# Strassen-Winograd halves in the MLP's second product: seven products instead of eight per quarter

## The chip, the cores and the metric

The kernel runs on one NeuronCore of a Trainium2 chip. Five engines work side by side, each through its own queue: TensorE (PE, matrix products; its weight loads are shown apart as PEld), VectorE (DVE), ScalarE (ACT), GpSimd (POOL) and SyncE (SP), which here issues the DMAs. They wait for each other through semaphores. The metric is the device time of one execution in microseconds, lower is better.

## The reference

A decoder block over 512 tokens of 1024 features: two attention-like branches are merged and added to the residual stream `x`, then an MLP with a squared ReLU, then gated input embeddings, then a last norm. What matters here is the part behind the branches:

```python
x = x + merged @ w_out[i]
h = rms_norm(x, mlp_norm_g[i])
x = x + jnp.square(jax.nn.relu(h @ w_ff1[i])) @ w_ff2[i]
gate = jax.nn.sigmoid(rms_norm(x, ple_norm_g[i]) @ w_ple_gate[i])
x = x + gate * (p[i] @ w_ple_proj[i])
...
return rms_norm(x, final_norm_g)
```

`w_ff1` is 1024 x 4096, `w_ff2` 4096 x 1024, all in float32.

## The kernel before

**Precision.** A float32 factor is split in two: `hi`, rounded by ScalarE to the short format that TensorE takes (fp32r), and `lo`, the remainder, by VectorE (`split`; for weights in `fetch_to`, L172 and L173). Every product is three matmuls: hi times hi, hi times lo, lo times hi.

**Weights** come in units of 128 x 1024 numbers (512 KB). The list `seq` (L126 to L145) fixes the order of all 132 units. `load_to` issues a unit's DMA on SyncE into `w_raw` (two buffers), `fetch_to` splits it into `w_hi` and `w_lo` (three buffers each). `weights(u, i)` takes the next unit; at the third `step()` within it, `fetch_to` prepares two units further on (L196).

**The MLP** (from L1081) runs in four quarters of 1024 hidden features. In a quarter, the first product makes eight tiles of 128 hidden features by 512 tokens, each from one unit of `U_FF1` (`product`, `mm3`, L188 to L190: 24 matmuls). `squared` (L1096) takes relu times the norm's factor on VectorE, the square on ScalarE, and splits the result into `f`. The second product, `by_token` with `U_FF2` (L1116), has 8 units for the quarter; for each half of 512 output columns, four units are multiplied with four tiles of 128 tokens (`rows3`, L203 to L205: 24 matmuls a unit, the activations stationary, 512 weight columns moving), and four VectorE additions put the sums from PSUM into `xs` (L1118). PSUM has eight banks of 128 x 512, taken in turn by `ps_main`.

**Around it.** Before the MLP, `embeddings(0, "mlp_g")` makes the first 512 columns of `p @ w_ple_proj` into the SBUF tile `ple`, two token tiles at a time, each pair followed by `gained`: 16 transposes on TensorE (L1021) and the splits of the transposed stream into `hx` (L1025, L1026). `norm_of` makes the norm's factors; `spread` (L1087) spreads them over partitions. Behind the MLP, `embeddings(1, "ple_g")` does the second half, and the gate's product (`U_GATE`) and the end follow. `wg`, a home for the last four split units of the gate, lies in the buffers of `f`.

**Order and memory.** The instructions of the text are put in order for each engine before the run, by readiness as a model of the program sees it and by the program's order; an engine then executes its list strictly in that order. A memory pool that is opened where a closed one lay waits until that one's tiles are done with.

Of the kernel before, what the change touches and what calls it, by code (L numbers as in the profile page):

```python
# [18 lines left out]
P = 128  # L19
T = 512  # L20
D = 1024
KT = D // P
# [25 lines left out]
NUNITS = _n  # L48
# [37 lines left out]
def tile_block(ctx: ExitStack, tc: tile.TileContext, xT, xt, pT, wts, lora, cols_d, gfin_d, consts_d, out, dbg=None):  # L86
    nc = tc.nc
    act, dve, pool, pe, sync = nc.scalar, nc.vector, nc.gpsimd, nc.tensor, nc.sync
# [7 lines left out]
    const = ctx.enter_context(tc.tile_pool(name="const", bufs=1))  # L96
    wpool = ctx.enter_context(tc.tile_pool(name="wpool", bufs=3))
    dpool = ctx.enter_context(tc.tile_pool(name="dpool", bufs=1, space=DRAM))

    o_sb = dpool.tile([P, HP, T], F32, name="o_sb")  # L100
    gates = dpool.tile([P, 2 * KT, T], F32, name="gates")
# [5 lines left out]
    omm = const.tile([P, 14], F32, name="omm")  # L107

    const.tile([P, PAD], F32, name="pad")
    w2a2 = const.tile([P, 512], F32, name="w2a2")  # L110
    g2 = const.tile([P, 512], F32, name="g2")

    def cc(k, w):
        return cst[:, COFF[k]:COFF[k] + w]
# [11 lines left out]
    seq = []  # L126
# [19 lines left out]
    assert len(seq) == NUNITS  # L146
    ready, loaded = {}, []
    state = {"i": 0, "used": 0, "due": 0}
    AHEAD = 3
    homes = {}  # L150

    def unit(i):
        return wts[UBASE[seq[i][0]] + seq[i][1]]

    def load_to(n):
        while len(loaded) < min(n, len(seq)):
            raw = wpool.tile([P, 1024], F32, name="w_raw", bufs=2)
            sync.dma_start(out=raw, in_=unit(len(loaded)))
            loaded.append(raw)

    def fetch_to(n, ahead=0):
        while state["i"] < min(n, len(seq)):
            i = state["i"]
            state["i"] += 1
            load_to(i + 1 + ahead)
            raw = loaded[i]
            if seq[i] in homes:
                hi, lo = homes[seq[i]]()
            else:
                hi = wpool.tile([P, 1024], F32R, name="w_hi")  # L170
                lo = wpool.tile([P, 1024], F32R, name="w_lo")
            act.copy(out=hi, in_=raw)  # L172
            dve.tensor_tensor(out=lo, in0=raw, in1=r32(hi), op=ALU.subtract)  # L173
            ready.setdefault(seq[i], []).append((hi, lo))

    def weights(u, i):
        assert seq[state["used"]] == (u, i), (seq[state["used"]], u, i)
        state["used"] += 1
        fetch_to(state["used"])
        state["due"] = 3  # L180
        return ready[(u, i)].pop(0)

    def mm3(ps, w, base, rhs, k, first, last, t=slice(0, T)):

# [13 lines left out]
    def rows3(ps, w, rhs, tt, k, first, last, cs=slice(0, 512)):  # L198

        xh, xl = (r[:, :, tt * P:(tt + 1) * P] for r in rhs)  # L200
        for j in range(2):
            wh, wl = (p_.rearrange("p (j f) -> p j f", j=2)[:, j, cs] for p_ in w)
            pe.matmul(ps, xh[:, k + j], wh, start=first and j == 0, stop=False)  # L203
            pe.matmul(ps, xh[:, k + j], wl, start=False, stop=False)  # L204
            pe.matmul(ps, xl[:, k + j], wh, start=False, stop=last and j == 1)  # L205
            step()

    def product(ps, w, rhs, nk=KT, base=0, t=slice(0, T)):
# [8 lines left out]
    def split(hi, lo, src):  # L217
        act.copy(out=hi, in_=src)
        dve.tensor_tensor(out=lo, in0=src, in1=r32(hi), op=ALU.subtract)
# [43 lines left out]
    pr = ctx.enter_context(tc.tile_pool(name="pr", bufs=1, side="right"))  # L263
    o_rw = pr.tile([P, HP, T], F32, name="o_rw")
# [4 lines left out]
    with ExitStack() as sA:  # L269
# [43 lines left out]
        with ExitStack() as s1:  # L313
# [12 lines left out]
            ps = ps_z()  # L326
# [41 lines left out]
            first = p1.tile([P, 4 * P], F32, name="first", tag="sums", bufs=1)  # L368
# [150 lines left out]
            pss = [psm.tile([P, T], F32, name="ps_m") for _ in range(2)]  # L519
# [15 lines left out]
                projected(0, i, pss[i])  # L535
            for _ in v:
                pass
            sync.dma_start(out=w2a2, in_=lora[:, 0:512])
            sync.dma_start(out=g2, in_=lora[:, 512:1024])

            def early():
                for hp in range(1, HP):
# [27 lines left out]
        with ExitStack() as s2:  # L570
# [423 lines left out]
    ple = px.tile([P, TT, D], F32, name="ple")  # L994
    pin = [px.tile([P, 2, T], F32R, name=f"pin{i}") for i in range(2)]
    px.tile([P, PADX], F32, name="padx")
    COLHALF = (slice(0, 512), slice(512, D))

    ps4 = ctx.enter_context(tc.tile_pool(name="ps4", bufs=6, space=PSUM))
# [14 lines left out]
    def gained(gname, half):  # L1014

        for kp in range(KT // 2):
            ps = ps_main().rearrange("p (j t) -> p j t", j=2)
            for j in range(2):
                for t in range(2):
                    k = kp * 2 + j  # L1020
                    pe.transpose(out=ps[:, j, t * P:(t + 1) * P], in_=xs[:, half * 2 + t, k * P:(k + 1) * P], identity=ident)  # L1021
            for j in range(2):
                k = kp * 2 + j
                t2 = slice(half * 256, half * 256 + 256)
                act.activation(out=hx[0][:, k, t2], in_=ps[:, j], func=AF.Copy, scale=col(gname, k))  # L1025
                dve.scalar_tensor_tensor(out=hx[1][:, k, t2], in0=ps[:, j], scalar=col(gname, k), in1=r32(hx[0][:, k, t2]),  # L1026
                                         op0=ALU.mult, op1=ALU.subtract)

    def embeddings(half, gname):

        pss = [ps_main() for _ in range(TT)]
        w = weights(U_PLE, half)
        for part in range(2):
            for tt in (part * 2, part * 2 + 1):
                rows3(pss[tt], w, pin, tt, 0, True, True)
                act.copy(out=ple[:, tt, COLHALF[half]], in_=pss[tt])
            gained(gname, part)

    def norm_of(pool_, name):

        st = pool_.tile([P, 3, TT], F32, name=name)
        sq = pool_.tile([P, D], F32, name="sqj", bufs=2)
        for tt in range(TT):
            act.activation(out=sq, in_=xs[:, tt, :], func=AF.Square, accum_out=st[:, 0, tt:tt + 1])
        dve.tensor_scalar(out=st[:, 0, :], in0=st[:, 0, :], scalar1=1.0 / D, scalar2=NORM_EPS, op0=ALU.mult, op1=ALU.add)
        root(st[:, 1, :], st[:, 2, :], st[:, 0, :])
        return st[:, 1, :]

    with ExitStack() as s3:
# [6 lines left out]
        for m in range(8):  # L1056
# [10 lines left out]
            ps = ps_main()  # L1067
# [10 lines left out]
    sP.close()  # L1078


    p4 = ctx.enter_context(tc.tile_pool(name="p4", bufs=1))  # L1081
    f = [p4.tile([P, KT, T], F32R, name=f"f{i}", tag=f"f{i}") for i in range(2)]
    embeddings(0, "mlp_g")
    r2 = norm_of(p4, "st2")
    rs2 = p4.tile([P, T], F32, name="rs2")

    def spread():  # L1087

# [4 lines left out]
            pe.matmul(ps[:, tt * P:(tt + 1) * P], onesd, dg, start=True, stop=True)  # L1093
        act.copy(out=rs2, in_=ps)

    def squared(ps, m):  # L1096
        r = p4.tile([P, T], F32, name="relu", bufs=3)
        dve.scalar_tensor_tensor(out=r, in0=ps, scalar=0.0, in1=rs2, op0=ALU.max, op1=ALU.mult)  # L1098
        act.activation(out=r, in_=r, func=AF.Square)
        split(f[0][:, m, :], f[1][:, m, :], r)  # L1100

    for qd in range(4):
        waiting = []
        for m in range(8):
            w = weights(U_FF1, qd * 8 + m)
            ps = ps_main()
            product(ps, w, hx)
            waiting.append((ps, m))
            if qd == 0 and m < 2:
                continue  # L1110
            if qd == 0 and m == 2:
                spread()
            while waiting:
                squared(*waiting.pop(0))
        for half in range(2):
            pss = by_token(U_FF2, qd * 8, f, half)  # L1116
            for tt in range(TT):
                dve.tensor_tensor(out=xs[:, tt, COLHALF[half]], in0=pss[tt], in1=xs[:, tt, COLHALF[half]], op=ALU.add)  # L1118


    gfin = p4.tile([P, D], F32, name="gfin")
    sync.dma_start(out=gfin, in_=gfin_d)
    wg = [p4.tile([P, 4, 1024], F32R, name=f"wg{i}", tag=f"f{i}") for i in range(2)]
    for kk in range(4):
        homes[(U_GATE, 4 + kk)] = lambda kk=kk: [t[:, kk, :] for t in wg]
# [116 lines left out]
```

## Time and profile before

| | us |
|---|---|
| median of 3 runs (911.72 to 912.33) | 912.2 |
| the profiled execution | 912.86 |
| its span, first to last instruction | 911.1 |
| first matmul of the MLP's second product, quarter 0 | 543.94 |
| end of the four quarters (first matmul of the embeddings' second half) | 848.58 |

A row of a group names line, engine, operation, output and inputs with their shapes, the count, busy time in us and the mean of one in ns, and the engine's idle time ahead of these with what ended it. A row of a stretch gives its bounds and length, then for PE, PEld, DVE, ACT and POOL the busy time with the number of instructions, the clock that TensorE was granted, the DMA engines' busy share and GB/s. A row in order of time gives start and duration in us, engine, line and operation, and in brackets the wait ahead of it. A row of a DMA gives the count, KB each and the median us from issue to landing. SPq is SyncE's queue.

### The profile page before, as it was taken

The page shows a single profiled execution, that of the slowest core. Times are in us where ns is not written, and L with a number is a line of the kernel's source. Part 1 is how long each engine was busy: PE and PEld are TensorE (multiplying, and loading weights), DVE is VectorE, ACT ScalarE, POOL GpSimd, SP SyncE. Part 2 cuts the span into 40 slices and gives each one's busy share as a digit, 9 for nine tenths or more (in the row PEclk, how much of TensorE's full clock was granted, in tenths as well). Part 3 has the DMA queues.
Part 4 walks back from the last instruction along what each step waited for, and adds up shares of the span by engine and source line. Part 5 has one row for each costly group of instructions (what it writes and reads, how often), then busy time and mean ns, then how long its engine had stood idle before and what let it go on. Part 6 is the DMA issues. An engine that isn't in the chain of part 4 may idle for free.

```text
span 911.1 us, 12423 instructions
## 1 busy us (share of the span) xinstructions
PE 893.6 (98%) x4758; PEld 724.3 (79%) x4758; DVE 576.7 (63%) x1086; ACT 416.0 (46%) x682; POOL 82.5 (9%) x137
## 2 busy tenths in 40 slices
PE   8999999999999999999999999999999999999995
PEld 5778788877787877877888888888888888888885
DVE  6899987886978969867835643344334334433666
ACT  6888878535336244344515441144123322321743
POOL 1333322003203112020000000000000000000000
PEclk9999999999999999999999999999999999999998
DMA  7221122220221223448732223332233322233222
GB/s 257 94 78 50 59 81 81 70 92 25 85 79 36 85 90 115 153 129 269 261 114 94 93 93 95 103 103 93 94 94 104 103 93 93 93 94 112 72 70 92
DMA packets 31306, 93.14 MB, mean 102 GB/s; under 512 B 3600, under 2 KB 3600, under 8 KB 31248
## 3 DMA queue, kind: packets, MB, share of 16 engines
q1 hardware_dynamic: 31248, 92.36, 30.9%
q8 instruction: 37, 0.61, 0.3%
q14 instruction: 21, 0.17, 0.1%
HBM read 82.91 MB, written 9.44 MB: 101 GB/s over the span
## 4 chain that ended last, share of the span: by engine, by line
PE 84%; DVE 8%; ACT 4%; DMA 2%; issue 1%; SPq 0%; POOL 0%; ACTq 0%; DVEq 0%
PE ps_m L188 14%; PE ps_m L189 14%; PE ps_m L190 14%; PE ps_m L203 9%; PE ps_m L204 9%; PE ps_m L205 9%; PE ps_g L807 2%; DVE w_lo L173 1%; PE ps_g L778 1%; PE ps_o L489 1%; PE ps_c L940 1%; PE ps_z L497 1%; PE ps_g L189 1%; PE ps_g L892 1%; PE ps_s L928 1%
## 5 line engine op out<-in xcount | busy, mean ns | idle before, releaser
L172 ACT CAST w_hi<-w_raw 128x1024 fp32r<-128x1024 f32 x126 | 132.7, 1053 | 323.3 <-PE ps_m L205 163.8
L173 DVE TENSOR_TENSOR w_lo<-w_raw,w_hi 128x1024 fp32r<-128x1024 f32 x126 | 154.5, 1226 | 141.3 <-ACT w_hi L172 141.0
L188 PE MATMUL ps_m<-h_hi,w_hi 128*128 128x512 f32 x320 | 129.7, 407 | 1.5 <-ACT h_hi L345 1.5
L189 PE MATMUL ps_m<-h_lo,w_hi 128*128 128x512 f32 x320 | 128.8, 402 | 0.0
L190 PE MATMUL ps_m<-h_hi,w_lo 128*128 128x512 f32 x320 | 128.6, 402 | 0.0
L188 PE MATMUL ps_m<-hx,w_hi 128*128 128x512 f32 x256 | 99.6, 390 | 0.5 <-ACT hx L1025 0.5
L189 PE MATMUL ps_m<-hx,w_hi 128*128 128x512 f32 x256 | 99.7, 390 | 0.0
L190 PE MATMUL ps_m<-hx,w_lo 128*128 128x512 f32 x256 | 99.6, 389 | 0.0
L203 PE MATMUL ps_m<-w_hi,f 128*128 128x512 f32 x256 | 99.6, 389 | 0.0
L204 PE MATMUL ps_m<-w_lo,f 128*128 128x512 f32 x256 | 99.6, 389 | 0.0
L205 PE MATMUL ps_m<-w_hi,f 128*128 128x512 f32 x256 | 99.6, 389 | 0.0
L188 PEld LDWEIGHTS ps_m<-h_hi,w_hi 128*128 128x128 f32 x320 | 60.7, 190 | 12.8 <-ACT h_hi L345 2.2
L1098 DVE SCALAR_TENSOR_TENSOR relu<-ps_m,rs 128x512 f32<-128x512 f32 x32 | 21.9, 691 | 76.7 <-PE ps_m L190 76.7
L190 PEld LDWEIGHTS ps_m<-h_hi,w_lo 128*128 128x128 f32 x320 | 60.2, 188 | 12.3
L189 PEld LDWEIGHTS ps_m<-h_lo,w_hi 128*128 128x128 f32 x320 | 60.3, 188 | 11.9 <-DVE h_lo L346 1.2
L188 PEld LDWEIGHTS ps_m<-hx,w_hi 128*128 128x128 f32 x256 | 48.0, 188 | 10.7 <-ACT hx L1025 0.8
L189 PEld LDWEIGHTS ps_m<-hx,w_hi 128*128 128x128 f32 x256 | 48.1, 188 | 10.2 <-DVE hx L1026 0.4
L205 PEld LDWEIGHTS ps_m<-w_hi,f 128*128 128x128 f32 x256 | 48.0, 188 | 10.1
L203 PEld LDWEIGHTS ps_m<-w_hi,f 128*128 128x128 f32 x256 | 48.0, 188 | 10.0
L190 PEld LDWEIGHTS ps_m<-hx,w_lo 128*128 128x128 f32 x256 | 48.0, 188 | 9.9
L204 PEld LDWEIGHTS ps_m<-w_lo,f 128*128 128x128 f32 x256 | 48.0, 188 | 9.9
L1118 DVE TENSOR_TENSOR xs<-ps_m,xs 128x512 f32<-128x512 f32 x32 | 21.3, 687 | 9.9 <-PE ps_m L205 9.9
(334 smaller groups left out, 1585.0 us busy)
## 6 DMA issues: line engine op xcount, KB each, us to landing
w_raw<-in_wts_dram SPq DMA_DIRECT2D x130, 512.0 KB, 3.3
gates<-gg SPq DMA_DIRECT2D x16, 256.0 KB, 2.0
x_in<-in_xT_dram SPq DMA_DIRECT2D x8, 256.0 KB, 6.3
tmp<-gates SPq DMA_DIRECT2D x8, 256.0 KB, 2.9
upsb<-tmp SPq DMA_DIRECT2D x8, 256.0 KB, 3.8
ga<-upsb SPq DMA_DIRECT2D x8, 256.0 KB, 4.9
gb<-gates SPq DMA_DIRECT2D x8, 256.0 KB, 5.1
xs<-in_xt_dram SPq DMA_DIRECT2D x4, 512.0 KB, 6.0
```

What stands on the lines that cost most here:

```text
L172: act.copy(out=hi, in_=raw)
L173: dve.tensor_tensor(out=lo, in0=raw, in1=r32(hi), op=ALU.subtract)
L188: pe.matmul(ps, wh, xh[:, k, t], start=first, stop=False)
L189: pe.matmul(ps, wh, xl[:, k, t], start=False, stop=False)
L190: pe.matmul(ps, wl, xh[:, k, t], start=False, stop=last)
L203: pe.matmul(ps, xh[:, k + j], wh, start=first and j == 0, stop=False)
L204: pe.matmul(ps, xh[:, k + j], wl, start=False, stop=False)
L205: pe.matmul(ps, xl[:, k + j], wh, start=False, stop=last and j == 1)
L489: pe.matmul(ps_o[:, j * P:T], vv[:, j, hh, :, :].rearrange("p a d -> p (a d)"), part[:, ZB[j]:ZB[j] + ZN[j]], start=j == 2 and part is wh, ...
L807: pe.matmul(ps[:, k], LB[:, k, :], rhs[:, k], start=True, stop=True)
L1098: dve.scalar_tensor_tensor(out=r, in0=ps, scalar=0.0, in1=rs2, op0=ALU.max, op1=ALU.mult)
L1118: dve.tensor_tensor(out=xs[:, tt, COLHALF[half]], in0=pss[tt], in1=xs[:, tt, COLHALF[half]], op=ALU.add)
```

## The change

The second product of a quarter is cut in halves: tokens (0 to 255, 256 to 511), hidden features (first and last 512 of the quarter) and output columns (first and last 512). With A the activations and B the weights, each a 2 x 2 of such halves, the eight products of halves become seven, after Winograd's form of Strassen's scheme: A11 B11, A12 B21, S2 T2, S1 T1, S3 T3, S4 B22, A22 T4, where S and T are sums of halves (as `LEFT`, `RIGHT` and the helpers have them). Results that several outputs share stay in PSUM (`V`, `W`) and are added to `xs` more than once.

- The sums of activations (S1 to S4) are made in `squared` by `minus` and `plus` on VectorE, 256 tokens wide, and split.
- The weights of a quarter are loaded as eight blocks `B11a` to `B22b`, at units 0 to 3 of the first product, into tiles of their own; T1 to T4 are made of them on VectorE, T2 and T3 in `sums_early` during the first product, T1 and T4 when units 4, 5, 7 and 8 of the second are fetched. The 14 units of the second product are split from these blocks.
- A product of halves (`seventh`) has 2 units, each for 2 token tiles: 12 matmuls a unit. Each is followed by two additions to `xs`.
- The first half of the embeddings goes to DRAM (`ple_d`) tile by tile and is read back behind the MLP.
- The MLP has a pool of its own, closed behind it; the tail's tiles lie in a new pool, `p5`. `pin` takes the place of `o_rw`, the joined `lora_w` is reused for `sums`, and `norm_of`'s scratch that of `T2a`.
- Behind the MLP, `gained` comes ahead of each pair of the embeddings' second half.

```diff
@@ sequence, weights
-        seq += [(U_FF2, qd * 8 + m) for m in range(8)]
+        seq += [(U_FF2, qd, i, p_) for i in range(7) for p_ in range(2)]
...
+            if seq[i][0] != U_FF2:
+                loaded[i] = wpool.tile([P, 1024], F32, name="w_raw", bufs=2)
+                sync.dma_start(out=loaded[i], in_=unit(i))
...
-            raw = loaded[i]
+            raw = loaded[i] if seq[i][0] != U_FF2 else sources[seq[i]]()
@@ embeddings
-    def embeddings(half, gname):
-
-        pss = [ps_main() for _ in range(TT)]
-        w = weights(U_PLE, half)
-        for part in range(2):
-            for tt in (part * 2, part * 2 + 1):
-                rows3(pss[tt], w, pin, tt, 0, True, True)
-                act.copy(out=ple[:, tt, COLHALF[half]], in_=pss[tt])
-            gained(gname, part)
+    def embeddings(tts, w, dst):
+
+        for tt in tts:
+            ps = ps_main()
+            rows3(ps, w, pin, tt, 0, True, True)
+            act.copy(out=dst(tt), in_=ps)
...
+    for half in range(2):
+        for tt in (half * 2, half * 2 + 1):
+            t = kept(tt)
+            embeddings((tt,), w, lambda tt: t)
+            sync.dma_start(out=ple_d[:, tt, :], in_=t)
+        gained("mlp_g", half)
@@ activations
+    LEFT = (fA11, part(fA2, 0), part(fS, 1), part(fS, 0), fS3, part(fS, 2), part(fA2, 1))
...
-        split(f[0][:, m, :], f[1][:, m, :], r)
+        sums = const.tile([P, 4, HT], F32, name="sums", tag="lora_w")
+        lo_, hi_ = r[:, 0:HT], r[:, HT:T]
+        if m < 4:
+            split(fA11[0][:, m], fA11[1][:, m], lo_)
+            minus(sums[:, 0], lo_, hi_)
+            split(fS3[0][:, m], fS3[1][:, m], sums[:, 0])
+        else:
+            k, low = m - 4, lower[m - 4]
+            split(fA2[0][:, k], fA2[1][:, k], r.rearrange("p (j t) -> p j t", j=2))
+            plus(sums[:, 1], low[:, HT:T], hi_)
+            minus(sums[:, 2], sums[:, 1], low[:, 0:HT])
+            minus(sums[:, 3], lo_, sums[:, 2])
+            split(fS[0][:, k], fS[1][:, k], sums[:, 1:4])
@@ weights' sums
+    def load_block(qd, n, p_):
+
+        i = {"B11": 0, "B21": 2, "B12": 4, "B22": 6}[n] + p_
+        t = blocks[n, p_] = p4.tile([P, 1024], F32, name=f"{n}{'ab'[p_]}")
+        sync.dma_start(out=t, in_=wts[UBASE[U_FF2] + qd * 8 + i])
+
+    def sums_early(p_):
+
+        minus(blocks["B12", p_], blocks["B22", p_], blocks["B12", p_])
+        blocks["T2", p_] = p4.tile([P, 1024], F32, name=f"T2{'ab'[p_]}")
+        plus(blocks["T2", p_], blocks["B12", p_], blocks["B11", p_])
+
+    def T1(p_):
+        minus(blocks["B11", p_], blocks["B22", p_], blocks["T2", p_])
+
+    def T4(p_):
+        minus(blocks["B21", p_], blocks["B21", p_], blocks["T2", p_])
+
+    RIGHT = ("B11", "B21", "T2", "B11", "B12", "B22", "B21")
+    BEFORE = {4: lambda: T1(0), 5: lambda: T1(1), 7: lambda: T4(0), 8: lambda: T4(1)}
...
+    LOADS = [[("B12", 0), ("B22", 0)], [("B11", 0), ("B12", 1)], [("B22", 1), ("B11", 1)], [("B21", 0), ("B21", 1)]]
@@ second product
+    def seventh(qd, i, pss):
+
+        op = LEFT[i]
+        first, last = pss is None, True
+        pss = pss or [ps_main() for _ in range(2)]
+        for p_ in range(2):
+            w = weights(U_FF2, qd, i, p_)
+            for t2 in range(2):
+                rows3(pss[t2], w, op, t2, p_ * 2, first and p_ == 0, p_ == 1)
+        return pss
...
-        for half in range(2):
-            pss = by_token(U_FF2, qd * 8, f, half)
-            for tt in range(TT):
-                dve.tensor_tensor(out=xs[:, tt, COLHALF[half]], in0=pss[tt], in1=xs[:, tt, COLHALF[half]], op=ALU.add)
+            if m in (2, 4):
+                sums_early(m // 2 - 1)
+        V = seventh(qd, 0, None)
+        to_x(V, 0, 0)
+        to_x(seventh(qd, 1, None), 0, 0)
+        V = seventh(qd, 2, V)
+        to_x(V, 0, 1)
+        W = seventh(qd, 3, None)
+        to_x(W, 1, 1)
+        V = seventh(qd, 4, V)
+        to_x(V, 1, 1)
+        W = seventh(qd, 5, W)
+        to_x(W, 0, 1)
+        V = seventh(qd, 6, V)
+        to_x(V, 1, 0)
@@ behind the MLP
+    sM.close()
+    p4 = ctx.enter_context(tc.tile_pool(name="p5", bufs=1))
+    wg = [p4.tile([P, 4, 1024], F32R, name=f"wg{i}") for i in range(2)]
...
+    ple = p4.tile([P, TT, D], F32, name="ple")
+    sync.dma_start(out=ple[:, :, COLHALF[0]], in_=ple_d)
...
-    embeddings(1, "ple_g")
+    w = weights(U_PLE, 1)
+    for half in range(2):
+        gained("ple_g", half)
+        embeddings((half * 2, half * 2 + 1), w, lambda tt: ple[:, tt, COLHALF[1]])
```

More of the change, by code (lines that the diff above doesn't have):

```diff
@@ L156, in load_to @@
         while len(loaded) < min(n, len(seq)):
-            raw = wpool.tile([P, 1024], F32, name="w_raw", bufs=2)
-            sync.dma_start(out=raw, in_=unit(len(loaded)))
-            loaded.append(raw)
+            i = len(loaded)
+            loaded.append(None)
+            if seq[i][0] != U_FF2:
+                loaded[i] = wpool.tile([P, 1024], F32, name="w_raw", bufs=2)
+                sync.dma_start(out=loaded[i], in_=unit(i))
     def fetch_to(n, ahead=0):
@@ L180, in weights @@
         state["due"] = 3
-        return ready[(u, i)].pop(0)
+        return ready[u].pop(0)
     def mm3(ps, w, base, rhs, k, first, last, t=slice(0, T)):
@@ L202, in rows3 @@
             wh, wl = (p_.rearrange("p (j f) -> p j f", j=2)[:, j, cs] for p_ in w)
-            pe.matmul(ps, xh[:, k + j], wh, start=first and j == 0, stop=False)
-            pe.matmul(ps, xh[:, k + j], wl, start=False, stop=False)
-            pe.matmul(ps, xl[:, k + j], wh, start=False, stop=last and j == 1)
+            pe.matmul(ps, xh[:, k + j], wh, start=first and j == 0, stop=False, skip_group_check=True)
+            pe.matmul(ps, xh[:, k + j], wl, start=False, stop=False, skip_group_check=True)
+            pe.matmul(ps, xl[:, k + j], wh, start=False, stop=last and j == 1, skip_group_check=True)
             step()
@@ L537, in tile_block @@
                 pass
-            sync.dma_start(out=w2a2, in_=lora[:, 0:512])
-            sync.dma_start(out=g2, in_=lora[:, 512:1024])
+            sync.dma_start(out=lora_w, in_=lora)
             def early():
@@ L993, in tile_block @@
     hx = [px.tile([P, KT, T], F32R, name=f"hx{i}") for i in range(2)]
-    ple = px.tile([P, TT, D], F32, name="ple")
-    pin = [px.tile([P, 2, T], F32R, name=f"pin{i}") for i in range(2)]
     px.tile([P, PADX], F32, name="padx")
+    pins = pr.tile([P, 2, 2, T], F32R, name="pins", tag="o_rw")
+    pin = [pins[:, i] for i in range(2)]
     COLHALF = (slice(0, 512), slice(512, D))
@@ L1094, in spread, with minus, plus @@
         act.copy(out=rs2, in_=ps)
+    def minus(out, a, b):
+        dve.tensor_tensor(out=out, in0=a, in1=b, op=ALU.subtract)
+    def plus(out, a, b):
+        dve.tensor_tensor(out=out, in0=a, in1=b, op=ALU.add)
+    lower = {}
     def squared(ps, m):
-        r = p4.tile([P, T], F32, name="relu", bufs=3)
+        if m < 4:
+            r = lower[m] = p4.tile([P, T], F32, name="rk", bufs=4)
+        else:
+            r = p4.tile([P, T], F32, name="r")
         dve.scalar_tensor_tensor(out=r, in0=ps, scalar=0.0, in1=rs2, op0=ALU.max, op1=ALU.mult)
@@ new lines, in T4, with source @@
+    def T4(p_):
+        minus(blocks["B21", p_], blocks["B21", p_], blocks["T2", p_])
+    RIGHT = ("B11", "B21", "T2", "B11", "B12", "B22", "B21")
+    BEFORE = {4: lambda: T1(0), 5: lambda: T1(1), 7: lambda: T4(0), 8: lambda: T4(1)}
+    for qd in range(4):
+        for i in range(7):
+            for p_ in range(2):
+                def source(i=i, p_=p_):
+                    BEFORE.get(2 * i + p_, lambda: None)()
+                    return blocks[RIGHT[i], p_]
+                sources[U_FF2, qd, i, p_] = source
@@ new lines, in tile_block, with to_x @@
+    LOADS = [[("B12", 0), ("B22", 0)], [("B11", 0), ("B12", 1)], [("B22", 1), ("B11", 1)], [("B21", 0), ("B21", 1)]]
[3 more added lines that the diff above has]
+        pss = pss or [ps_main() for _ in range(2)]
+        for p_ in range(2):
+            w = weights(U_FF2, qd, i, p_)
+            for t2 in range(2):
+                rows3(pss[t2], w, op, t2, p_ * 2, first and p_ == 0, p_ == 1)
+        return pss
+    def to_x(pss, th, half):
+        for t2 in range(2):
+            xb = xs[:, th * 2 + t2, COLHALF[half]]
+            dve.tensor_tensor(out=xb, in0=pss[t2], in1=xb, op=ALU.add)
@@ L1105, in tile_block @@
             w = weights(U_FF1, qd * 8 + m)
+            for l in LOADS[m] if m < 4 else ():
+                load_block(qd, l[0], l[1])
             ps = ps_main()
```

38 lines of the change are left out of this document (25 added, 13 removed).

## The prediction

> **What bounds the kernel now.** First the page: the engines' totals, the chain that ended last, and the three groups of the product that is changed.
>
> ```profile
> span 911.1 us, 12423 instructions
> PE 893.6 (98%) x4758; PEld 724.3 (79%) x4758; DVE 576.7 (63%) x1086; ACT 416.0 (46%) x682; POOL 82.5 (9%) x137
> PE 84%; DVE 8%; ACT 4%; DMA 2%; issue 1%; SPq 0%; POOL 0%; ACTq 0%; DVEq 0%
> L203 PE MATMUL ps_m<-w_hi,f 128*128 128x512 f32 x256 | 99.6, 389 | 0.0
> L204 PE MATMUL ps_m<-w_lo,f 128*128 128x512 f32 x256 | 99.6, 389 | 0.0
> L205 PE MATMUL ps_m<-w_hi,f 128*128 128x512 f32 x256 | 99.6, 389 | 0.0
> ```
>
> TensorE is busy 98% of the span and the chain lies on it: a matmul less should be time less. How much is not the 389 ns of the groups, since a matmul starts before the one ahead has ended. So next TensorE in order of time where the second product of quarter 0 (L203 to L205) begins and where the next quarter's first product (L188 to L190) follows it (start, duration, engine, line); then the MLP's stretches, with engines' busy time and counts, and at the top one from the merge with a loaded VectorE.
>
> ```profile
> 543.94 0.39 PE L203 MATMUL ps_m<-w_hi,f 128*128 128x512 f32 x1
> 544.16 0.39 PE L204 MATMUL ps_m<-w_lo,f 128*128 128x512 f32 x1
> ...
> 587.23 0.39 PE L205 MATMUL ps_m<-w_hi,f 128*128 128x512 f32 x1
> 587.46 0.39 PE L188 MATMUL ps_m<-hx,w_hi 128*128 128x512 f32 x1
> ```
>
> ```profile
> 430.00:455.00 25.00, 25.00 (x112) 20.67 (x112) 20.93 (x28) 13.15 (x19) 0.00 (x0) 1.00 0.82 281
> 543.94:587.46 43.52, 43.52 (x194) 36.04 (x192) 15.62 (x17) 9.57 (x10) 0.00 (x0) 1.00 0.30 97
> 587.46:630.98 43.52, 43.52 (x194) 36.04 (x192) 19.91 (x23) 16.55 (x23) 0.00 (x0) 1.00 0.31 97
> ```
>
> The second product of a quarter is 8 units x 24 = 192 matmuls, from 543.94 to 587.46: 43.52 / 192 = 0.2267 us from start to start. TensorE never waits there, at full clock (1.00). In the top row VectorE is busy 20.93 of 25 us and DMA 0.82, and TensorE still starts 112 matmuls in 25 us: a loaded VectorE doesn't slow matmuls that have their operands. A quarter is 87.04 us, of which VectorE is busy 15.62 + 19.91 = 35.5 us.
>
> **What is removed.** A product of halves is 2 weight units x 2 token tiles x 6 = 24 matmuls, seven of them 168 instead of 192. The four quarters lose 4 x 24 = 96 matmuls of the same shape: 96 x 0.2267 = **21.8 us**, on the path. The Trainium skill ("TensorE: Matmul & The Clock Gate", Back-to-back issue gap) gives 512 / 2.4 + 2.5 = 215.7 ns for this gap; by it the gain would be 20.7 us; the trace has 226.7 ns for these very matmuls and decides.
>
> **What is added, and what covers it.** A unit now lasts TensorE 12 x 0.2267 = 2.72 us instead of 5.44, while each unit still needs ScalarE's rounding (L172) and VectorE's remainder (L173). The rows: costs in the first product's stretch, then 256-wide VectorE work, then both engines in time from 543.9 on.
>
> ```profile
> L173 DVE TENSOR_TENSOR w_lo<-w_raw,w_hi 128x1024 fp32r<-128x1024 f32 x8 | 9.8, 1225 | 1.6 <-ACT w_hi L172 1.6
> L172 ACT CAST w_hi<-w_raw 128x1024 fp32r<-128x1024 f32 x9 | 9.5, 1055 | 30.9 <-PE ps_m L189 26.6 <-PE ps_m L205 4.4
> L219 DVE TENSOR_TENSOR f<-relu,f 128x512 fp32r<-128x512 f32 x7 | 4.8, 693 | 0.0
> L1098 DVE SCALAR_TENSOR_TENSOR relu<-ps_m,rs 128x512 f32<-128x512 f32 x7 | 4.8, 692 | 19.3 <-PE ps_m L190 19.3
> L1118 DVE TENSOR_TENSOR xs<-ps_m,xs 128x512 f32<-128x512 f32 x7 | 4.6, 687 | 1.8 <-PE ps_m L205 1.8
> L1137 DVE TENSOR_TENSOR xs<-xs,t 128x256 f32<-128x256 f32 x2 | 0.8, 425 | 0.0
> L1136 DVE TENSOR_TENSOR t<-t,ple 128x256 f32<-128x256 f32 x2 | 0.8, 416 | 0.0
> ```
>
> ```profile
> 543.91 1.05 ACT L172 CAST w_hi<-w_raw 128x1024 fp32r<-128x1024 f32 x1 [3.20 <-PE ps_m L189]
> 549.58 1.05 ACT L172 CAST w_hi<-w_raw 128x1024 fp32r<-128x1024 f32 x1 [3.43 <-PE ps_m L205]
> ...
> 544.14 0.69 DVE L1098 SCALAR_TENSOR_TENSOR relu<-ps_m,rs 128x512 f32<-128x512 f32 x1 [2.70 <-PE ps_m L190]
> 545.00 1.23 DVE L173 TENSOR_TENSOR w_lo<-w_raw,w_hi 128x1024 fp32r<-128x1024 f32 x1 [0.17 <-ACT w_hi L172]
> 546.18 0.69 DVE L219 TENSOR_TENSOR f<-relu,f 128x512 fp32r<-128x512 f32 x1
> 561.54 1.23 DVE L173 TENSOR_TENSOR w_lo<-w_raw,w_hi 128x1024 fp32r<-128x1024 f32 x1 [4.22 <-ACT w_hi L172]
> 562.69 1.28 DVE L1118 TENSOR_TENSOR xs<-ps_m,xs 128x512 f32<-128x512 f32 x2
> ```
>
> VectorE per quarter afterwards: 22 weight remainders (8 + 14) x 1.225 = 27.0; 8 sums of weight blocks (two inputs, 1024 wide: the L173 row is nearest) x 1.225 = 9.8; 8 relu 5.5; 14 additions to xs instead of 8, x 0.687 = 9.6; 4 remainders of 512, 2.8; 24 operations of 256 (4 x 3 for the lower rows, 4 x 3 for the upper) x 0.42 = 10.1; 4 remainders of 768, for which no row exists: between 0.69 and 1.23 each, I take the middle, 0.96, 3.8. Sum 68.6 us, in a quarter of 81.6 (43.52 + 168 x 0.2267 = 38.1). ScalarE stays near half. So no engine passes TensorE over a quarter. The tight place is the second product: 14 remainders 17.2 + 14 additions 9.6 + 4 block sums (T1, T4) 4.9 + the tail of the last relu 3.6 (0.69 + 0.69 + 3 x 0.42 + 0.96) = **35.3 of 38.1 us**.
>
> The Trainium skill ("VectorE: DVE Perf Modes", The DRAIN you can't avoid) says that an operation doesn't start before the pipe of the one ahead is empty, which speaks against this change, with its many more operations; by it the 35.3 us is what counts. The trace has a remainder at 561.54 and the next operation 1.15 us later, within its 1.23: a little less.
>
> Does a weight come late? Three buffers: unit i+2 may be rounded when unit i-1 is done (the waits on L205 and L189 in the rows), which leaves two units, 2 x 2.72 = **5.44 us**, before it is needed. In this time: the additions of the product just done, ready 0.2 us after its end (2 x 0.69 = 1.38), one block sum (1.23), the remainder of the unit before (1.23) and its own (1.23); the rounding (1.05) runs beside the additions on ScalarE. 0.2 + 1.38 + 3 x 1.23 = **5.3 us** when all fall together, which they don't at most units: only four of 14 have a block sum. So no wait, with 0.1 us to spare in the worst place and 2.7 us at most. Cost taken 0, bounds 0 to 1.4 us a quarter (second rival). The first units after the turn from first to second product: relu, square, rounding and remainders as in the rows took from 544.14 to 546.87; unit 2's remainder lay between, done at 546.23, 2.3 us after the turn; it will be due 5.44 us after. The last relu's two-way sums (0.42 x 3 + 0.96 behind ScalarE's square and roundings) end about 6.5 us after the turn; S2 is due after two products, 10.9 us. PSUM: V, W and one product hold six of eight banks, each read by the time that its turn comes again.
>
> **The moved parts.** Their rows: the embeddings before the first quarter, SyncE's queue, a rounding, a ScalarE wait for a load, VectorE's first split for hx; then TensorE at the end of the MLP.
>
> ```profile
> 489.63 0.33 SPq L1122 DMA_DIRECT2D gfin<-in_gfin_dram  x1
> 491.98 65.71 SPq L158 DMA_DIRECT2D w_raw<-in_wts_dram  x12
> ...
> 499.10 0.74 PE L188 MATMUL ps_m<-hx,w_hi 128*128 128x512 f32 x2 [0.53 <-ACT hx L1025]
> 505.60 1.05 ACT L172 CAST w_hi<-w_raw 128x1024 fp32r<-128x1024 f32 x1 [2.02 <-PE ps_m L189]
> ...
> 420.54 0.63 ACT L1064 ACTIVATE gb<-gb 128x512 f32<-128x512 f32 x1 [3.16 <-DMA gb<-gates]
> 494.14 1.66 DVE L1026 SCALAR_TENSOR_TENSOR hx<-ps_m,cols,hx 128x256 fp32r<-128x256 f32 x4 [2.19 <-ACT hx L1025]
> ```
>
> ```profile
> 848.58 0.39 PE L203 MATMUL ps_m<-w_hi,pin 128*128 128x512 f32 x1
> 851.30 1.91 PE L1021 MATMUL ps_m<-cst,xs 128*128 128x128 f32 x16
> 852.97 0.48 PE L203 MATMUL ps_m<-w_hi,pin 128*128 128x512 f32 x1
> 857.45 0.48 PE L203 MATMUL ps_m<-w_hi,hx 128*128 128x512 f32 x1
> ```
>
> ```profile
> w_raw<-in_wts_dram SPq DMA_DIRECT2D x130, 512.0 KB, 3.3
> xs<-in_xt_dram SPq DMA_DIRECT2D x4, 512.0 KB, 6.0
> gfin<-in_gfin_dram SPq DMA_DIRECT2D x1, 512.0 KB, 3.6
> ```
>
> The load of gfin, written behind all four quarters, was issued at 489.63, when the MLP's memory came free: loads don't keep the program's place. So the eight weight blocks of quarter 0 (4.2 MB) may all be issued there, ahead of the raw load at 491.98 (unit 3 of the first product). At the 281 GB/s of the busiest stretch the nine take 16.8 us: landed by about 508.8 instead of 495.3, rounded and subtracted by 511.3 (in ScalarE's row its rounding began at 505.60); TensorE needs it at 499.1 + 3 x 5.44 + 0.7 (L1093's matmuls) = 516. Cost 0; the cover is 4.7 us. The four 256 KB stores to DRAM go through the same queue; their buffers are wanted at 517. In later quarters the blocks are the same 512 KB units as before, only earlier. TensorE's order in this stretch is unchanged, the wait of 0.53 us stays.
>
> Block sums can come early too, and then VectorE stands still for a load behind its queue, as ScalarE did for gb (3.16 us at 420.54). Behind the waiting sum stand the splits for hx, for which TensorE waits at 499.1. VectorE's gap ahead of 494.14 is 2.19 us, two sums long. Sums of the first three blocks, landed by 489.6 + 1.4 + 3 x 1.87 = 496.6 (512 KB at 281 GB/s is 1.87 us, 1.4 the rest of the 3.3), would end at 497.8: the splits start 3.7 us late, eight of 0.41 us and one more end at 501.5 instead of 499.2, and TensorE starts 2.3 us late. If the sum with the sixth block (502.2) stands ahead as well, 5 us. Bounds 0 and 5 us, once; I take **1.5 us**, nearer 2.3 than 0, since the gap fits.
>
> At the end of the MLP TensorE does the same 24 matmuls and 32 transposes (848.58 to 857.45, 8.87 us), transposes first: these need tokens 0 to 255, whose last addition follows the sixth product, 5.44 us earlier; and V's two additions hide under them. The pool for the tail opens only when the MLP's is done, so the reload of 1 MB and gfin stand on SyncE's queue ahead of the raw load of U_GATE 2: 6.0 (two 512 KB, by the xs row) + 3.6 + 3.3 = 12.9 us after the end, while TensorE wants that unit at 8.87 + 2 x 5.44 = 19.8, less 2.3 for splitting. Cover 4.6 us. The row sums of squares, which began before the end, move behind it; they are wanted only at the gate's sigmoid, over 20 us later. The joined load of lora_w is early and awaited by nobody near: 0.
>
> **Sum.** 912.86 (profiled execution; span 911.1) - 21.8 + 1.5 = **892.6 us**. That execution is 0.66 us above the median of the runs, so theirs should lie at 891.9 to 892.6; I say 892.5.
>
> **Rivals.**
> 1. *VectorE and ScalarE work in series (slower).* If a unit's rounding waits behind VectorE's queue as well (block sum, rounding, remainder one after the other, since both read one block), a product takes 2 x (1.05 + 1.23) + 1.38 + 4/7 x 1.23 + some 0.4 of handing over = 7.0 us instead of 5.44: 28 x 1.6 = 45 us, 937 us. It turns slower from 21.8 / 28 = 0.78 us of wait a product. For it: 35.3 of 38.1. Against it: in the rows rounding starts as its buffer comes free, and only four units a quarter have a sum. 0.09.
> 2. *Waits at the turn only.* The first two products (10.9 us) meet the tail 3.6, two block sums 2.45, four remainders 4.9 and two additions 1.38 on VectorE: 12.3 us. If the sums T1 come ahead of the remainders, unit 4 is late by 1.4 us in each quarter: 5.7 us, 898.3, and with the 5 us above 901.8. For it: VectorE executes in one order. Against: T1 can be done earlier, in the first product. 0.20.
> 3. *It is worth the busy time*, 96 x 0.389 = 37.3 us, 877: the 0.2267 us between starts speaks against it. 0.02.
> 4. *It does not do what it says:* the weights' pace, not TensorE, sets the second product so that seven products take as long as eight, 912: 35.3 is under 38.1 and far under 43.5. 0.03.
>
> **Chances and range.** The forecast, 889 to 895, has 0.66, the rivals 0.09, 0.20, 0.02, 0.03. About 0.2% (1.8 us) is what can be told from no change. Faster 0.88, same 0.03, slower 0.09. The range 888.5 to 902 leaves out rivals 1, 3 and 4, 0.14; its low end is the sum without the 1.5 us and the 0.66, with 2 us for the bounds of stages (the 0.53 us wait among them).
>
> **What would show it.** Right: TensorE's second product of a quarter 38.1 us from first to last start, at 0.2267 us a matmul, no wait of PE on w_lo or fS; 96 matmuls fewer; VectorE near 69 us a quarter; 8.9 us at the end. Wrong: starts of matmuls apart by more than 0.23 us at unit bounds with a wait on DVE L173 (rivals 1, 2) or on a DMA; a wait for hx past 499 (the block sums); a slower pitch inside a unit, which nothing here foresees.

## The result, and the profile after

| | us |
|---|---|
| median after, 4 runs (890.04 to 891.51) | 890.33 |
| median before, 4 runs of the same session (911.72 to 912.34) | 912.27 |
| ratio after to before | 0.9763, 95% interval 0.9746 to 0.9780 |
| profiled execution after | 890.04 |

The kernel became 21.9 us faster; 892.5 was forecast, and the result lies inside the forecast's range. First the page of after: span, engines' totals, the chain that ended last by engine, and two groups of the changed product.

```profile
span 888.3 us, 12491 instructions
PE 871.9 (98%) x4662; PEld 706.5 (80%) x4662; DVE 689.4 (78%) x1262; ACT 456.7 (51%) x738; POOL 82.7 (9%) x137
PE 83%; DVE 9%; ACT 5%; DMA 1%; issue 1%; SPq 0%; POOL 0%; DVEq 0%; ACTq 0%
L206 PE MATMUL ps_m<-w_hi,fS 128*128 128x512 f32 x128 | 49.8, 389 | 0.0
L206 PE MATMUL ps_m<-w_hi,fA 128*128 128x512 f32 x96 | 37.3, 389 | 0.0
```

TensorE has 4758 - 4662 = 96 matmuls less, and is as before busy 98% of the span, although VectorE went from 576.7 to 689.4 us. The idle time ahead of the groups is 0.0. Where the time went is read from TensorE in order of time (start, duration, engine, line).

```profile
498.02 0.73 PE L191 MATMUL ps_m<-hx,w_hi 128*128 128x512 f32 x2 [0.40 <-ACT hx L1027]
542.94 0.39 PE L206 MATMUL ps_m<-w_hi,fA 128*128 128x512 f32 x1
580.79 0.39 PE L208 MATMUL ps_m<-w_hi,fA 128*128 128x512 f32 x1
581.02 0.39 PE L191 MATMUL ps_m<-hx,w_hi 128*128 128x512 f32 x1
825.82 1.91 PE L1023 MATMUL ps_m<-cst,xs 128*128 128x128 f32 x16
834.91 0.39 PE L206 MATMUL ps_m<-w_hi,hx 128*128 128x512 f32 x1
```

The four quarters last from 498.02 to 825.82, 327.80 us, where they took 499.10 to 848.58, 349.48 us: 21.68 us less. Ahead of them the span lost 1.08 us (499.10 to 498.02), behind them 0.04 (911.1 - 848.58 = 62.52; 888.3 - 825.82 = 62.48): together the 22.8 us between the two spans. The 1.08 us isn't the change's: 1.07 of it is there already at the first matmul of the embeddings, in before and then in after:

```profile
489.44 0.39 PE L203 MATMUL ps_m<-w_hi,pin 128*128 128x512 f32 x1
```

```profile
488.37 0.39 PE L206 MATMUL ps_m<-w_hi,pins 128*128 128x512 f32 x1
```

From there to the MLP's first matmul it is 9.66 and 9.65 us. Of the change, only the joined load of `lora_w` and new places in memory lie ahead of that matmul, and one execution differs from another there: in the profiled executions of the kernels below it starts anywhere from 488.18 to 490.44.

The stretches of after: second product of quarter 0, first and second product of quarter 1, second product of quarter 3, then the embeddings' second half (columns as in the prediction's stretches).

```profile
542.94:581.02 38.08, 38.08 (x170) 31.54 (x168) 34.31 (x40) 17.42 (x18) 0.00 (x0) 1.00 0.39 125
581.02:624.54 43.52, 43.52 (x194) 36.05 (x192) 29.35 (x46) 18.98 (x29) 0.00 (x0) 1.00 0.27 85
624.54:662.63 38.09, 38.09 (x170) 31.55 (x169) 33.28 (x39) 17.42 (x18) 0.00 (x0) 1.00 0.36 117
787.75:825.85 38.10, 38.10 (x170) 31.51 (x169) 30.78 (x37) 17.41 (x18) 0.00 (x0) 1.00 0.04 15
825.85:834.91 9.06, 9.06 (x57) 7.93 (x56) 7.49 (x17) 8.84 (x21) 0.00 (x0) 1.00 0.78 278
```

A second product lasts 38.08 to 38.10 us instead of 43.52: 5.43 us less, four times. 38.08 / 168 = 0.2267 us a matmul, the pitch of before, at full clock and without a wait. VectorE is busy 34.31 of 38.08 us there (15.62 of 43.52 before).

### The profile page after: what moved, and what is told of

Read it like the earlier page. It is cut to its first block, busy times and chain, and to the rows that moved or that the text cites. A ratio compares the mean times of both kernels' runs of the same rounds, so it can differ in the third digit from the quotient of the medians.

```text
span 888.3 us, 12491 instructions
## 1 busy us (share of the span) xinstructions
PE 871.9 (98%) x4662; PEld 706.5 (80%) x4662; DVE 689.4 (78%) x1262; ACT 456.7 (51%) x738; POOL 82.7 (9%) x137
## 4 chain that ended last, share of the span: by engine, by line
PE 83%; DVE 9%; ACT 5%; DMA 1%; issue 1%; SPq 0%; POOL 0%; DVEq 0%; ACTq 0%
PE ps_m L191 14%; PE ps_m L192 14%; PE ps_m L193 14%; PE ps_m L208 9%; PE ps_m L207 9%; PE ps_m L206 9%; PE ps_g L809 2%; DVE w_lo L176 1%; PE ps_g L780 1%; PE ps_g L192 1%; PE ps_g L193 1%; PE ps_c L942 1%; PE ps_o L492 1%; PE ps_g L191 1%; PE ps_s L930 1%
## 5 line engine op out<-in xcount | busy, mean ns | idle before, releaser
L175 ACT CAST w_hi<-w_raw 128x1024 fp32r<-128x1024 f32 x94 | 99.2, 1055 | 152.8 <-PE ps_m L192 95.1
L176 DVE TENSOR_TENSOR w_lo<-w_raw,w_hi 128x1024 fp32r<-128x1024 f32 x94 | 115.2, 1226 | 35.5 <-ACT w_hi L175 35.2
L206 PE MATMUL ps_m<-w_hi,fS 128*128 128x512 f32 x128 | 49.8, 389 | 0.0
L207 PE MATMUL ps_m<-w_lo,fS 128*128 128x512 f32 x128 | 49.8, 389 | 0.0
L208 PE MATMUL ps_m<-w_hi,fS 128*128 128x512 f32 x128 | 49.8, 389 | 0.0
L208 PE MATMUL ps_m<-w_hi,fA 128*128 128x512 f32 x96 | 37.3, 389 | 0.0
L206 PE MATMUL ps_m<-w_hi,fA 128*128 128x512 f32 x96 | 37.3, 389 | 0.0
L207 PE MATMUL ps_m<-w_lo,fA 128*128 128x512 f32 x96 | 37.3, 389 | 0.0
L221 ACT CAST fS<-sums 128x256 fp32r<-128x256 f32 (+1 forms) x32 | 19.9, 622 | 33.2 <-DVE sums L1119 33.2
L1192 DVE TENSOR_TENSOR xs<-ps_m,xs 128x512 f32<-128x512 f32 x56 | 35.9, 684 | 0.0
```

The source lines that it names most:

```text
L207: pe.matmul(ps, xh[:, k + j], wl, start=False, stop=False, skip_group_check=True)
L1192: dve.tensor_tensor(out=xb, in0=pss[t2], in1=xb, op=ALU.add)
```

## The experiments

Theory: the change is worth 96 pitches of 0.2267 us, and nothing else in it costs or brings time. Rivals: another part of it brings or takes time (the pool, the order behind the MLP); preparing the weights is so near its limit that the room left is luck; a matmul is worth something else than its pitch. The kernels of two sessions were each compared with before there (medians 911.92 and 912.12 us).

### The seventh product once more (e1, e1b)

In e1 the matmuls of the seventh product run a second time with the same operands, into two spare banks that nobody reads. So TensorE has its 96 matmuls back, and all other work of the change stays.

```diff
@@ seventh, for each unit, behind rows3
+            if i == 6:
+                spare = spare if p_ else [ps_main() for _ in range(2)]
+                for t2 in range(2):
+                    xh, xl = (r[:, :, t2 * P:(t2 + 1) * P] for r in op)
+                    for j in range(2):
+                        wh, wl = (q.rearrange("p (j f) -> p j f", j=2)[:, j] for q in w)
+                        for n, (a, b) in enumerate(((xh, wh), (xh, wl), (xl, wh))):
+                            pe.matmul(spare[t2], a[:, p_ * 2 + j], b, start=p_ + j + n == 0, stop=p_ + j == 2 and n == 2, skip_group_check=True)
```

> The changed kernel with the eighth product put back on TensorE alone: in the seventh product of each quarter every unit's 12 matmuls run once more into two spare PSUM banks that nobody reads; no weight, sum or addition is added. Theory (a matmul is worth the 0.2267 us between starts): 96 matmuls more, +21.8 us, 912.1, and a second product of 43.5 us. Rival 3 (it is worth its busy 389 ns): +37.3, 927.6. Rival 4 (the weights' pace sets the second product): the extra matmuls fit into waits, +0 to +5.

Measured: 911.97 us, ratio to before 1.0001 (0.9992 to 1.0011). Its second product of quarter 0:

```profile
543.93:587.45 43.52, 43.52 (x194) 36.04 (x192) 36.19 (x42) 17.38 (x18) 0.00 (x0) 1.00 0.36 121
```

The 43.52 us are back to the last digit, with VectorE as loaded as in after (36.19 us). Its MLP lasts 349.52 us (499.05 to 848.57) against 327.80: 21.72 / 96 = 0.2263 us a matmul. So TensorE sets the second product, and the whole gain lies in these 96 matmuls.

e1b puts bf16 matmuls of the same shape there, on a constant, dead as well: does the pitch hang on the format?

```diff
@@ seventh, for each unit, behind rows3
+            if i == 6:
+                spare = spare if p_ else [ps_main() for _ in range(2)]
+                for n in range(12):
+                    a, b = cst.bitcast(BF16)[:, 0:P], cst.bitcast(BF16)[:, 512:1024]
+                    pe.matmul(spare[n % 2], a, b, start=p_ == 0 and n < 2, stop=p_ == 1 and n > 9, skip_group_check=True)
```

> As e1_eighth, but the 24 extra matmuls per quarter are of bf16 operands, 128 x 128 by 512 columns, into spare banks. If the 0.2267 us are the cost of any matmul here: starts 0.2267 us apart, +21.8. If the Trainium skill's 215.7 ns (TensorE: Matmul & The Clock Gate, Back-to-back issue gap, bf16) holds and the rest is the fp32r format's: 0.2157 us apart, +20.7; to be read from the starts in the trace rather than from the time.

One run: 913.2 us. It began its MLP late, at 500.09 (its granted clock was 0.58 from 9.49 to 13.60 us, where after's was 1.00), and ended it at 848.99: 348.90 us, 21.10 more than after, 0.2198 us for each of the 96 with the changes of format between. One unit's twelve in e1b, with the fp32r matmuls behind them:

```profile
585.71 2.76 PE L1192 MATMUL ps_m<-cst 128*128 128x512 bf16 x12
588.12 0.58 PE L191 MATMUL ps_m<-hx,w_hi 128*128 128x512 f32 x1
588.54 0.40 PE L192 MATMUL ps_m<-hx,w_hi 128*128 128x512 f32 x1
```

The first fp32r matmul behind them starts early in the record and is long (0.58); counted to the second, less one pitch, the twelve take 588.54 - 585.71 - 0.2267 = 2.60 us, 0.217 each. Single starts inside these units, which the row merges, lie 0.2158 us apart (mean of 80 spacings). The isolated gap that the Trainium skill gives ("TensorE: Matmul & The Clock Gate", Back-to-back issue gap: N / 2.4 + 2.5 ns, 215.8 ns for 512 columns) fits these, and not the kernel's own fp32r matmuls.

### All but the seven products (e2)

Eight products as before (`f` in two tiles, the eight units, `by_token` and four additions), and the rest of the change: embeddings through DRAM, the MLP's pool, the order behind it.

```diff
-        seq += [(U_FF2, qd, i, p_) for i in range(7) for p_ in range(2)]
+        seq += [(U_FF2, qd * 8 + m) for m in range(8)]
...
-            raw = loaded[i] if seq[i][0] != U_FF2 else sources[seq[i]]()
+            raw = loaded[i]
...
+        for half in range(2):
+            pss = by_token(U_FF2, qd * 8, f, half)
```

> Everything of the change but the seven products: eight products as before, with the embeddings' first half through DRAM, the MLP's own pool, the new places of pin, lora_w and the scratch, and transposes first behind the MLP. Theory: the moved parts cost and bring nothing, 912.3 within 1 us. Rival: they are a part of the gain or hide a loss: under 911 or over 913.5.

Measured: 912.56 us, ratio 1.0006 (0.9997 to 1.0016). The moved parts neither cost nor bring anything that shows: by the interval, they cost 1.5 us at the most and bring 0.3.

### One buffer less for the split weights (e3)

One of the three buffers of `w_hi` and of `w_lo` is held through the MLP, so a unit can be prepared one unit ahead instead of two: half of the lead on which the prediction's "no wait" stands.

```diff
@@ ahead of the quarters
+    hold = [wpool.tile([P, 1024], F32R, name=n) for n in ("w_hi", "w_lo")]
+    for t in hold:
+        dve.memset(r32(t)[:, 0:1], 0.0)
@@ behind them
+    for t in hold:
+        dve.tensor_tensor(out=xs[:, 3, 0:1], in0=r32(t)[:, 0:1], in1=xs[:, 3, 0:1], op=ALU.add)
```

> The changed kernel with one of the three buffers for split weights held through the MLP, so that a unit's rounding starts one unit ahead instead of two. Theory (the lead of 5.44 us covers rounding, remainder and VectorE's queue): with 2.72 us the chain 1.05 + 1.23 fits only where VectorE is free; at the turn (about 3 us), at four block sums (about 1 us each) and at some additions TensorE waits, 5 to 9 us a quarter, 910 to 926. If the lead is not what covers it: 890.3.

Measured: 898.49 us, ratio 0.9858 (0.9842 to 0.9873), 8.2 us over after: less than expected. A row of the view of waits (total us, times and longest), one of TensorE in order of time, and the stretch of quarter 0:

```profile
PE ps_m L207 <- DVE w_lo L176: 3.6, 8, 1.7
```

```profile
550.97 0.50 PE L207 MATMUL ps_m<-w_lo,fA 128*128 128x512 f32 x1 [0.30 <-DVE w_lo L176]
```

```profile
544.47:584.22 39.75, 39.22 (x170) 31.18 (x169) 34.87 (x40) 17.00 (x18) 0.00 (x0) 1.00 0.32 105
```

TensorE now waits for the remainders, which it never does in after, but only eight times. The listed 3.6 us are less than the loss: the matmul at 550.97 starts 0.69 us after the one ahead (550.28) instead of 0.23, and the next (551.31) 0.34 after it, together 0.58 us lost where 0.30 is listed. The MLP as a whole, 335.95 us (499.60 to 835.55), is 8.15 longer than after's. The rounding (1.05) and the remainder (1.15 to the next operation) fit into one unit of 2.72 us where nothing else stands in VectorE's queue. Seven of the waits, 0.2 to 0.3 us each, are for units behind other sums and additions. The longest is of another kind: VectorE stood still 2.63 us ahead of a block sum for the next quarter, whose load had not landed, and the remainder came behind it.

```profile
661.17 1.23 DVE L1119 TENSOR_TENSOR B12a<-B22a,B12a 128x1024 f32<-128x1024 f32 x1 [2.63 <-DMA B22a<-in_wts_dram]
663.58 0.50 PE L207 MATMUL ps_m<-w_lo,fA 128*128 128x512 f32 x1 [1.72 <-DVE w_lo L176]
```

The profiled execution (900.7 us) is the slowest of the four; whether the others have this long wait is not known.

### More work for VectorE (e4a, e4b)

The remainder of a unit is computed twice, with the same result: in e4a for half of the 14 units (the diff), in e4b, without the second condition, for all. (Two lines are added there, so L206 of after is L208.)

```diff
@@ fetch_to, behind the subtraction
+            if seq[i][0] == U_FF2 and seq[i][3] == 0:
+                dve.tensor_tensor(out=lo, in0=raw, in1=r32(hi), op=ALU.subtract)
```

> The changed kernel with the remainder of the first unit of every product of halves computed twice on VectorE (7 a quarter more, 1.14 us from start to start each, 8.0 us). VectorE was busy 33.3 to 34.3 of 38.1 us in the second product, 4.6 of it block sums of the next quarter that can go later. Theory (VectorE has room, but least at the turn): 33.8 - 4.6 + 8 = 37.2 still fits; T2's first unit, ready 0.65 us ahead of its use, comes behind two more remainders, 2.3 us: TensorE waits 1.6 to 4 us a quarter, 897 to 906. Theory of an ample cover: 890.3.

> As e4a_half, with the remainder of all 14 units computed twice, 16.0 us a quarter more on VectorE. Theory: 33.8 - 4.6 + 16 = 45.2 us of VectorE for 38.1 of TensorE: VectorE sets the pace of the second product, 7 us a quarter and more, 918 to 930, slower than before the change (rival 1's end by another cause). If only the chain of one unit counted (1.05 + 2.4 in 5.44): 890.3.

Measured: e4a 899.15 us, 0.9857 (0.9842 to 0.9872); e4b 924.07 us, 1.0127 (1.0112 to 1.0143), slower than before. Waits and second product of quarter 0, e4a and then e4b:

```profile
PE ps_m L208 <- ACT w_hi L175: 3.0, 4, 0.7
PE ps_m L209 <- DVE w_lo L178: 2.5, 4, 0.7
```

```profile
542.71:583.04 40.33, 38.85 (x170) 31.23 (x168) 39.70 (x46) 17.40 (x18) 0.00 (x0) 1.00 0.36 110
```

```profile
PE ps_m L209 <- DVE w_lo L178: 17.6, 21, 2.3
```

```profile
543.32:590.48 47.16, 41.97 (x170) 32.08 (x168) 45.14 (x51) 17.27 (x18) 0.00 (x0) 0.96 0.29 92
```

In e4a VectorE is busy 39.70 of 40.33 us (98%), in e4b 45.14 of 47.16: it has become the bound of this stretch. The four waits listed for ScalarE in e4a don't speak against that. TensorE's list is in another order here, as in e3: where a remainder comes late, two to four matmuls on `w_hi` stand ahead of the unit's first on `w_lo`, where in after the two alternate. So at 554.98 a matmul of the next product stands ahead of T2a's first on `w_lo` and waits for the rounding of B11a, which ends at 554.93; the remainder that comes behind it, T2a's second, ends at 555.50 in any case. Seven remainders a quarter (7 x 1.15 = 8 us) lengthen the kernel by 8.8 us, 2.2 a quarter, so about 5.8 of the 8 still found room; fourteen (16 us) by 33.7 us, 8.4 a quarter (0.8 of it at half clock, see the last section), so of the second 8 us 6.2 were paid. The room of VectorE behind the change is some 6 to 8 us a quarter, and most of what lies above it is paid.

### The order behind the MLP (e6)

```diff
     for half in range(2):
-        gained("ple_g", half)
         embeddings((half * 2, half * 2 + 1), w, lambda tt: ple[:, tt, COLHALF[1]])
+        gained("ple_g", half)
```

> The changed kernel with the old order behind the MLP: each pair of the embeddings' second half ahead of its transposes. Theory: the 24 matmuls and 32 transposes are the same and nothing waits: 890.3 within 1 us. Rival: the transposes first are worth the cover of hx: +1 to +2 us.

Measured: 890.06 us, 0.9763 (0.9747 to 0.9779): as after. Transposes first or embeddings first makes no difference here; the last addition to `xs` is not late either way.

## Why the prediction was right

**The 21.8 us.** 96 pitches of 0.2267 us; measured 21.68 between the two MLPs, 21.94 between the medians, and 21.72 when e1 took it back. The choice that mattered was to price a matmul by its distance to the next start, not by its 389 ns.

**No wait in the second product.** It held, though the tightest place is not the one for which the sum was made. "0.1 us to spare in the worst place" was said of a unit behind two additions and a block sum; in all four quarters the tightest unit is T2a's, the first of the third product, behind the work of the turn, with 0.87 us to spare. VectorE's list around the turn in after, then this unit's first matmul and the first one that reads the remainder:

```profile
543.37 0.69 DVE L1131 SCALAR_TENSOR_TENSOR r<-ps_m,rs 128x512 f32<-128x512 f32 x1
543.99 1.22 DVE L176 TENSOR_TENSOR w_lo<-B21a,w_hi 128x1024 fp32r<-128x1024 f32 x1
...
546.94 1.22 DVE L1119 TENSOR_TENSOR B21a<-B21a,T2a 128x1024 f32<-128x1024 f32 x1
...
551.08 0.95 DVE L222 TENSOR_TENSOR fS<-sums,fS 128x768 fp32r<-128x768 f32 x1
551.95 1.22 DVE L176 TENSOR_TENSOR w_lo<-T2a,w_hi 128x1024 fp32r<-128x1024 f32 x1
```

```profile
553.82 0.39 PE L206 MATMUL ps_m<-w_hi,fS 128*128 128x512 f32 x1
554.04 0.39 PE L207 MATMUL ps_m<-w_lo,fS 128*128 128x512 f32 x1
```

The remainder of T2a ends at 553.17. The matmul at 553.82 reads `w_hi` alone (the 0.65 us of e4a's expectation are counted to it); the remainder is read at 554.04, 0.87 us later. S2's last split ends at 552.03, 8.7 us after the last relu at 543.37, where "about 6.5 us after the turn" was said (9.1 after it). So the second rival had the right place: a sum of blocks stands ahead of the remainders (T4 at 546.94, wanted only in the seventh product). One of T1's sums in the same place, 1.14 us to the next operation, would have been too much for the 0.87; both had been made in the first product. The prediction had named that against this rival, but had not worked out the order, so the margin is in part luck. The last of the two sums in after:

```profile
541.24 1.23 DVE L1119 TENSOR_TENSOR B11b<-B22b,T2b 128x1024 f32<-128x1024 f32 x1
```

**VectorE's load.** 68.6 us a quarter was said; 29.35 + 33.28 = 62.6 measured, mostly because an operation starts before the one ahead has ended: the durations in these two stretches add up to 67.2 (the remainder at 543.99 and the next at 545.14 are 1.15 us apart at 1.22 us each, as in the trace of before). The split of 768, taken at 0.96 without a row, took 0.95. In the second product 35.3 of 38.1 was said, and 30.8 to 34.3 measured; T1's two sums have moved ahead of it, and in three of four quarters the next quarter's four stand in it.

**The 1.5 us for early block sums was the term that failed**: it measured 0. Loads and sums were indeed early, as said, but not in one burst. SyncE's queue, and VectorE ahead of the first quarter, in after:

```profile
488.56 0.33 SPq L1153 DMA_DIRECT2D B12a<-in_wts_dram  x1
...
499.01 0.60 SPq L1153 DMA_DIRECT2D B21a<-in_wts_dram  x1
503.77 0.33 SPq L162 DMA_DIRECT2D w_raw<-in_wts_dram  x1
504.14 0.43 SPq L1153 DMA_DIRECT2D B21b<-in_wts_dram  x1
```

```profile
493.07 1.66 DVE L1028 SCALAR_TENSOR_TENSOR hx<-ps_m,cols,hx 128x256 fp32r<-128x256 f32 x4 [2.19 <-ACT hx L1027]
494.89 1.27 DVE L1028 SCALAR_TENSOR_TENSOR hx<-ps_m,cols,hx 128x256 fp32r<-128x256 f32 x3 [0.17 <-ACT hx L1027]
496.08 1.22 DVE L1119 TENSOR_TENSOR B12a<-B22a,B12a 128x1024 f32<-128x1024 f32 x1
```

The eight loads lie between 488.56 and 504.14, with the stores and two raw loads between them. The first sum stands behind the first seven splits for `hx`, not in the gap of 2.19 us ahead of them, and VectorE doesn't wait for its blocks. TensorE's wait for `hx` ahead of the MLP is 0.40 us instead of 0.53, and the way from the embeddings to the MLP is as long as before (9.65 and 9.66 us; 9.42 in e2, which has no block sums: 0 to 0.23 us for them).

In later quarters, where the prediction put nothing for the blocks ("only earlier"), the same mechanism does occur. In quarter 1's second product of after, VectorE stands still for a block of quarter 2, with the remainder of B21a behind it:

```profile
653.76 1.23 DVE L1119 TENSOR_TENSOR B12a<-B22a,B12a 128x1024 f32<-128x1024 f32 x1 [1.04 <-DMA B22a<-in_wts_dram]
```

It costs no time here, because that remainder still has 1.3 us to spare (2.4 in quarter 0); with one buffer less, in e3, the same place made the longest wait.

**The rivals.** The fourth (the weights' pace sets the second product) and the third (a matmul is worth its busy time) fell with e1. The first, VectorE and ScalarE in series, is not what happens even with half the lead: e3 lost 8.2 us, where 45 were worked out for it. Its end on the slower side exists, though: with 16 us more on VectorE a quarter the change would have cost 11.95 us (924.07 against 912.12). By e4b the loss per product is 33.7 / 28 = 1.2 us, above the 0.78 us from which that rival was to decide; by e4a 8.8 / 28 = 0.31, below it.

**The end of the MLP** took 9.06 us instead of 8.87, and TensorE waited for no raw load of `U_GATE` behind it.

## What to carry to other kernels

Where TensorE is never idle, price a removed matmul by the distance between starts in that stretch, and then ask whether the engine that prepares the operands still fits into the shorter time: here seven products for eight were affordable because VectorE had been busy only 15.62 of 43.52 us. The margin is read at the tightest unit (0.87 us here), not from the sum of busy time, and it is worth a run that loads the preparing engine more, to know how far off the turn is. Seven products might serve the gate's or the output's product too; this wasn't tried, and VectorE's room there is not known.

## What the runs showed of the hardware that was not expected

**A wait can cost twice.** e4b's stretch has a clock of 0.96. In order of time around its longest wait, and the stretches there:

```profile
569.38 0.39 PE L208 MATMUL ps_m<-w_hi,fS 128*128 128x512 f32 x1
572.01 0.50 PE L209 MATMUL ps_m<-w_lo,fS 128*128 128x512 f32 x1 [2.24 <-DVE w_lo L178]
...
573.27 0.62 PE L209 MATMUL ps_m<-w_lo,fS 128*128 128x512 f32 x1
573.69 0.63 PE L210 MATMUL ps_m<-w_hi,fS 128*128 128x512 f32 x1
...
576.67 0.40 PE L208 MATMUL ps_m<-w_hi,fS 128*128 128x512 f32 x1
```

```profile
572.01:573.27 1.26, 1.26 (x5) 1.04 (x6) 1.26 (x2) 0.00 (x0) 0.00 (x0) 1.00 0.35 49
573.27:576.67 3.40, 3.40 (x9) 2.66 (x8) 2.15 (x3) 0.99 (x1) 0.00 (x0) 0.50 0.75 261
```

1.26 us after a wait of 2.24 us, the granted clock fell to half for 3.40 us, and eight matmuls took 0.425 us each to the next start: 8 x 0.198 = 1.6 us more. Of the four such waits, one a quarter, two were followed by it (2.24 and 2.12 us) and two were not (2.25 us each). In the other eight traces the granted clock is full throughout the MLP. The Trainium skill ("TensorE: Matmul & The Clock Gate", What's actually happening) says that the gate goes to half after an idle window of about 3.4 us, in a window that runs free of the program; the 3.40 us at half clock and the two of four fit this, but 2.24 us of waiting were enough here.

**The distance between fp32r matmuls seems to have a fixed part at full clock.** Beside the 512-wide ones at 0.2267 us, the gate's end in after has a run of 256-wide ones:

```profile
872.99 0.28 PE L206 MATMUL ps_m<-wg,hx 128*128 128x256 f32 x1
...
878.50 0.28 PE L207 MATMUL ps_m<-wg,hx 128*128 128x256 f32 x1
```

They are 47 rows, 5.51 / 46 = 0.1198 us apart. If the distance is a fixed part and a part that grows with the width, two such against one of 512 leave 2 x 0.1198 - 0.2267 = 0.013 us a matmul for the fixed part. bf16 in e1b, at 0.2158 us, leaves 0.002 for it, and at half clock the 0.425 us leave no room for it (0.2267 - 0.013 = 0.214, twice that is 0.427). What it is was not tried.
